# A hybrid attention block with a gated MLP on one core: stick-breaking products moved a chunk behind their transposes, MLP operands combined in rows, first loads of the down product moved into the last up block

## The chip, the core and the metric

The kernel runs on one core of one Trainium2 chip. The core has a tensor engine (TensorE, PE in the profile, with its weight loads shown apart as PEld), a vector engine (VectorE, DVE), a scalar engine (ScalarE, ACT), GpSimd (POOL) and a queue engine (SyncE, SP) which here issues nearly all transfers. The engines run their own instruction lists in order and wait for each other on semaphores. Matrix products land in PSUM, which the kernel uses as eight banks of 128 partitions by 512 float32; everything else on the core lies in SBUF.

The metric is the device time of one execution in microseconds; lower is better. One execution was also recorded by the hardware profiler, and all durations below come from that one.

## What is computed

One decoder layer over 1024 rows of width 1024: a norm, one projection, sparse attention on eight heads and stick-breaking attention on eight others, a norm by head, an output projection with residual, a second norm, a gated MLP with a causal convolution of width 3, and a last norm. The parts that the change touches, cut from the reference:

```python
def _rms_norm(x, w):
    y = xf * lax.rsqrt(jnp.mean(xf * xf, axis=-1, keepdims=True) + EPS)
    return (y * w).astype(x.dtype)
...
def _stick_breaking(q, k, v):            # 8 heads of width 64, T = 1024
    for nb in range(T // QBLK):          # QBLK = 128 rows of q
        z = jnp.einsum('bhqd,bhkd->bhqk', qb, kb) * scale
        log_rest = jnp.where(mask, jax.nn.log_sigmoid(-z), 0.0)
        after = lax.cumsum(log_rest, axis=3, reverse=True) - log_rest
        a = jnp.where(mask, jnp.exp(jax.nn.log_sigmoid(z) + after), 0.0)
        outs.append(jnp.einsum('bhqk,bhkd->bhqd', a, vb))
...
h = h + mixed @ w_out[layer]
u = _rms_norm(h, norm2_w[layer])
up = u @ w_up[layer]                     # 1024 -> 2 x 2816
up = conv_width_3(up, conv_w[layer]) + conv_b[layer]
gate, val = up[..., :D_FF], up[..., D_FF:]
h = h + (jax.nn.silu(gate) * val) @ w_down[layer]
return _rms_norm(h, final_norm_w)
```

## The kernel before

All matrices are float32. A factor is split into a high part (a copy rounded to the reduced type that PE multiplies fast, `fp32r` in the rows) and a low part (factor minus high part), and a product is three matmuls: high by high, high by low, low by high. Splitting a weight is `split_w` (lines 190 to 193): ACT copies, GpSimd subtracts (VectorE for the activations of the down product). Splitting what comes out of a PE transpose is `evac_hl` (lines 180 to 188): ACT copies from PSUM, VectorE subtracts from PSUM.

The code is written as generators that are pulled in turn, so that the work of one stage is emitted between the instructions of another; a scheduler then fixes each engine's order. PSUM tiles have tags: `tr` (two banks, for transposes), `z` (three banks), `o`, `ma` and `mb` (one bank each).

**Stick-breaking attention** (`sb_attend`, lines 367 to 401). There are four pairs of heads, two heads in each, four pairs of row blocks in each head, and the key blocks are cut into chunks of at most four. One turn of the loop pulls `sb_front` of chunk i and `sb_back` of chunk i - 2 (`SB_LAG`), together with projections that serve as filling. `sb_front` makes the logits (lines 422 to 425), ACT takes two sigmoids from the bank, VectorE scans one of them into a running product (line 433) and GpSimd multiplies (line 436) into `A`. `sb_back` takes each pair of key blocks of `A`: four transposes into a `tr` bank (line 463), `evac_hl` into `ph` (ACT, line 184) and `pl` (VectorE, line 185), three buffers each, and then the products with `V` into `o` (lines 453 and 455), in the order ph, pl, ph, pl. The products of one pair of key blocks are emitted after the transposes of the next pair, those of the chunk's last pair after one pull more. When a row block is done, ACT copies `o` (line 481) and `finish` transposes it (line 497) and VectorE reduces the bank into `osb` (line 498). Norms by head come from `head_norm_steps`, whose root is `rstd` (line 162) with `pool` set: GpSimd scales (line 168) and raises to the power -1/2 (line 169).

Right behind it come the blocks of the compressed keys (VectorE line 598, PE line 603) and `project_v` (line 1181), whose raw weights go through the tiles `na` and `nb` of the pool `nt`. The first four raw loads (lines 1192 and 1193) are issued between 19 and 31 us.

**MLP.** The up product is done with seven block products instead of eight, on combinations of the four quarters of its operand (the first and second half of the rows, each by the first and second half of the width): P1 and P2 are the two quarters of rows 0 to 511, and P6, P7, P5, P4 and P3 are sums and differences of quarters. `mlp` (lines 1209 to 1336) does the output projection by row blocks; `row` (line 1268) normalises a row block into a tile `un` (four buffers) without the weight of the norm. `first_half` transposes the first four row blocks (line 1234, eight groups of four transposes), scales by the norm's weight in the copies (lines 187, 188 and 1243) and keeps a float32 copy `bf`. `second_half` has four turns: two groups of transposes, three combinations on VectorE (lines 1255, 1257 and 1259) and one on GpSimd (line 1261), five copies on ACT (line 1264) and five subtractions (line 1265), three on VectorE and two on GpSimd, all from SBUF. It is pulled between the products P1 and P2 of the first three blocks of the up product, the lead products; the rest of the up product runs in `up` (22 blocks, seven products of twelve matmuls each, lines 1392 to 1394).

**Down product** (`down`, lines 1470 to 1567). It goes over two halves of the rows, each with eight banks of sums. The first group has three weight blocks, whose weights and activations are loaded before it; the activations of blocks 0 to 2 use tiles of the up product's pool `gran`. Behind the group the pools of the up product close, the pool `dp` opens in their place, and the loads of block 3 on go there: `ar` for the raw activation (line 1492), `ah` and `al` for its parts. The activation of each up block goes to `act_d` in HBM (line 1423) and is read back from there.

## Time and profile before

| what | us |
|---|---|
| median of three runs (lowest, highest) | 1510.08 (1509.42, 1510.47) |
| the profiled execution, by the same clock | 1511.7 |
| span of its trace, first to last instruction | 1510.0 |
| PE busy in the span | 1440.7 (95%) |
| DVE, ACT, POOL busy | 989.5, 804.8, 776.2 |

The stages by time in the trace: the first norm and projections up to about 60 us, stick-breaking attention with its filling to 372, the projections of the sparse attention to 440, sparse attention to 700, the output projection to 813.6, then a stretch in which the operands of the up product are made while the lead products run, to about 900, the up product to 1258, the down product to 1503 and a tail.

PE busy counts a pipelined matmul from its start to a modelled end, so matmuls of 0.39 us start every 0.23 us when they stand in a row, and a short pause between two does not show as idle time. What PE loses is read from the times at which its matmuls start, from the rows on waits (of PE and of its weight loads), and from the granted clock, which is 1.00 in a stretch at 2.4 GHz and 0.50 at 1.2 GHz.

### The profile page before, as it was taken

How to read it: one execution, taken by the hardware profiler on the slowest of the kernel's cores; microseconds unless marked ns; L12 is line 12 of the kernel's file. 1: busy time of each engine (PE TensorE's matmuls, PEld its weight loads, DVE VectorE, ACT ScalarE, POOL GpSimd, SP SyncE). 2: the span in 40 equal slices, each digit the busy share in tenths (PEclk: the TensorE clock that was granted, in tenths of full speed). 3: DMA queues.
4: the chain of work that ended last, by engine and by line, in shares of the span. 5: the costliest groups of instructions: out<-in, count | busy, mean ns of one | idle time of the engine just before them, and what ended most of it. 6: DMA issues, size and time to landing. Idle time of an engine off the chain costs nothing. (4 is left out here: it accounts for less than half of the span.)

```text
span 1510.0 us, 21800 instructions
## 1 busy us (share of the span) xinstructions
PE 1440.7 (95%) x7571; PEld 1201.5 (80%) x7571; DVE 989.5 (66%) x2013; ACT 804.8 (53%) x1705; POOL 776.2 (51%) x739
## 2 busy tenths in 40 slices
PE   7999999988999999999999799999999999999998
PEld 5777787777987988998888578888888887888886
DVE  5576777676337899998435897777777775614112
ACT  5565666553458888887416444444444453424122
POOL 3344555544336567665133856666666662645043
PEclk8999999999999999999999999999999999999999
DMA  6201101121331010003340122222222223845321
GB/s 208 70 15 28 29 15 28 47 67 53 99 94 29 1 57 2 1 16 105 113 126 35 58 96 79 82 84 85 84 84 84 83 93 130 287 147 181 109 95 56
DMA packets 111402, 119.10 MB, mean 79 GB/s; under 512 B 6860, under 2 KB 84156, under 8 KB 110908
## 3 DMA queue, kind: packets, MB, share of 16 engines
q1 hardware_dynamic: 111292, 117.71, 24.2%
q8 instruction: 60, 0.98, 0.3%
q14 instruction: 50, 0.41, 0.1%
HBM read 93.98 MB, written 23.70 MB: 78 GB/s over the span
## 5 line engine op out<-in xcount | busy, mean ns | idle before, releaser
L436 POOL TENSOR_TENSOR A<-A,tt 128x384 f32<-128x384 f32 (+3 forms) x96 | 90.4, 946 | 125.6 <-DVE tt L433 84.8
L193 POOL TENSOR_TENSOR gl<-mxs,gh 128x512 fp32r<-128x512 f32 x88 | 114.8, 1304 | 61.7 <-ACT gh L192 57.7
L193 POOL TENSOR_TENSOR gl<-wr,gh 128x512 fp32r<-128x512 f32 x66 | 86.1, 1306 | 94.9 <-ACT gh L192 65.8
L193 DVE TENSOR_TENSOR al<-ar,ah 128x512 fp32r<-128x512 f32 x41 | 49.1, 1214 | 126.3 <-ACT ah L192 121.6
L185 DVE TENSOR_TENSOR pl<-ps_tr,ph 128x512 fp32r<-128x512 f32 (+1 forms) x175 | 111.6, 641 | 17.1 <-ACT ph L184 15.4
L193 POOL TENSOR_TENSOR dl<-wr,dh 128x1024 fp32r<-128x1024 f32 x28 | 70.6, 2529 | 98.8 <-ACT dh L192 89.7
L184 ACT ACTIVATE ph<-ps_tr 128x512 fp32r<-128x512 f32 (+1 forms) x175 | 97.8, 563 | 42.6 <-PE ps_tr L463 24.4
L192 ACT ACTIVATE gh<-mxs 128x512 fp32r<-128x512 f32 x91 | 57.3, 629 | 75.6 <-PE ps_ma L1393 22.8
L433 DVE TENSOR_TENSOR_SCAN tt<-tt 128x384 f32<-128x384 f32 (+1 forms) x64 | 67.7, 1061 | 34.2 <-ACT tt L426 33.4
L192 ACT ACTIVATE ah<-ar 128x512 fp32r<-128x512 f32 x41 | 25.7, 629 | 111.2 <-PE ps_ma L1525 101.4
L193 POOL TENSOR_TENSOR wl<-wr,wh 128x512 fp32r<-128x512 f32 x40 | 54.7, 1371 | 50.4 <-ACT wh L192 50.4
L426 ACT ACTIVATE tt<-ps_z 128x384 f32<-128x384 f32 (+3 forms) x96 | 47.8, 497 | 40.3 <-PE ps_z L423 24.2
L692 POOL TENSOR_SCALAR lgw<-lgw,r,gates 128x640 f32<-128x640 f32 (+4 forms) x64 | 48.5, 767 | 39.3 <-DVE r L690 20.8
L192 ACT ACTIVATE gh<-wr 128x512 fp32r<-128x512 f32 x66 | 40.9, 624 | 43.9 <-DMA wr<-w_up_d 15.0
L218 PE MATMUL ps_ma<-uh,wh 128*128 128x512 f32 x136 | 59.4, 437 | 0.3 <-DVE mts L299 0.3
L219 PE MATMUL ps_ma<-ul,wh 128*128 128x512 f32 x136 | 54.7, 402 | 2.8 <-DVE ul L188 2.8
L220 PE MATMUL ps_ma<-uh,wl 128*128 128x512 f32 x136 | 54.2, 398 | 0.0
L463 PE MATMUL ps_tr<-ident,A 128*128 128x128 f32 x320 | 48.2, 274 | 3.8 <-DVE osb L498 3.1
L455 PE MATMUL ps_o<-pl,V 128*128 128x256 f32 x160 | 45.7, 307 | 5.2 <-DVE pl L185 3.3
L218 PE MATMUL ps_mb<-late,wh 128*128 128x512 f32 x120 | 50.4, 420 | 0.0
L463 PEld LDWEIGHTS ps_tr<-ident,A 128*128 128x128 f32 x320 | 37.6, 140 | 13.0 <-DVE osb L498 5.0
L427 ACT ACTIVATE A<-ps_z 128x384 f32<-128x384 f32 (+3 forms) x96 | 47.8, 498 | 0.1
(686 smaller groups left out, 5229.4 us busy)
## 6 DMA issues: line engine op xcount, KB each, us to landing
wr<-w_up_d SPq DMA_DIRECT2D x44, 512.0 KB
wr<-w_down_d SPq DMA_DIRECT2D x36, 512.0 KB
act_d<-na SPq DMA_DIRECT2D x44, 256.0 KB
ar<-act_d SPq DMA_DIRECT2D x41, 256.0 KB
wr<-w_in_d SPq DMA_DIRECT2D x40, 256.0 KB
...
```

The lines of the kernel that those rows point to most:

```text
L184: nc.scalar.activation(hi, src, AF.Copy)
L185: nc.vector.tensor_sub(lo, src, f(hi))
L192: nc.scalar.activation(hi, raw, AF.Copy)
L193: (eng or nc.gpsimd).tensor_sub(lo, raw, f(hi))
L218: nc.tensor.matmul(out, lh, rh, start=(i == 0), stop=False)
L219: nc.tensor.matmul(out, lh, rl, start=False, stop=False)
L220: nc.tensor.matmul(out, ll, rh, start=False, stop=(i == last))
L426: nc.scalar.activation(tt[:, 0:w], z[:, :w], AF.Sigmoid, scale=-1.0)
L433: nc.vector.tensor_tensor_scan(rev, rev, rev, 1.0 if carry[j] is None else carry[j], op0=ALU.mult, op1=ALU.bypass)
L436: nc.gpsimd.tensor_mul(A[:, j, 0:w], A[:, j, 0:w], tt[:, 1:w + 1])
L463: nc.tensor.transpose(pt[:, kk * 256 + j * P:kk * 256 + (j + 1) * P], A[:, j, c0:c0 + P], self.ident)
L692: nc.gpsimd.tensor_scalar(lg[i][:, :L], lg[i][:, :L], r[:, i:i + 1], gate[:, i:i + 1], op0=ALU.mult, op1=ALU.mult)
```

## The change

Nothing is altered in what is computed; the norm's weight is multiplied in another place.

1. *Stick-breaking.* `sb_back` is cut in two: `sb_turn` does the transposes and `evac_hl` of chunk i - 2, and the new `sb_back` does the products of chunk i - 3, all pairs of key blocks of the chunk, in the order ph, ph, pl, pl. `ph` and `pl` have five buffers instead of three, and the loop has one turn more.
2. *MLP operands in rows.* The norm's weight is loaded as a row broadcast to 128 partitions, in the tiles `na` and `nb`; `row` multiplies it in. All eight `un` tiles are kept, `bf` is gone. The new `combine` makes the sums and differences on the row tiles, four subtractions of 128 by 512 on VectorE for each of four pairs of row blocks, in place (one into `mxs`). Every one of the seven operands is then transposed by itself, in four groups of four transposes, each split by `evac_hl` from PSUM: 28 groups of transposes in place of 16. Four groups are pulled between lead products where one turn of `second_half` was.
3. *Down product.* The first group has four weight blocks instead of three. Their weights and activations are loaded within the last up block, the activations' parts into the tiles of P7.

```diff
-        for i in range(len(units) + self.SB_LAG):
+        for i in range(len(units) + self.SB_LAG + 1):
...
+            for lag, step in ((self.SB_LAG, self.sb_turn), (self.SB_LAG + 1, self.sb_back)):
+                if lag <= i < len(units) + lag:
+                    unit = units[i - lag]
+                    p = unit[0]["p"]
+                    gens.append(step(ops[p], work, unit, osb[p], mx, p, aux))
...
-            ph = self.tl(work, [P, 512], "ph", 3, F32R)
-            pl = self.tl(work, [P, 512], "pl", 3, F32R)
+            ph = self.tl(work, [P, 512], "ph", 5, F32R)
+            pl = self.tl(work, [P, 512], "pl", 5, F32R)
             self.evac_hl(ph, pl, pt)
...
+        for k0, ph, pl in u[b1]:
+            yield
+            for half in (ph, pl):
+                for kk in range(2):
+                    nc.tensor.matmul(o[:, :256], V[:, k0 + kk, :], half[:, kk * 256:kk * 256 + 256],
+                                     start=first and k0 == b1 - 2 and kk == 0 and half is ph,
+                                     stop=k0 == 0 and kk == 1 and half is pl)
...
+        w2 = [self.tl(self.nt, [P, 512], t, 2) for t in ("na", "nb")]
...
+        def operand(name, pieces):
+
+            hi, lo = R[name]
+            for k in range(4):
+                pt = self.ps("tr")
+                for j in range(4):
+                    nc.tensor.transpose(pt[:, j * P:(j + 1) * P], pieces(j, k), self.ident)
+                self.evac_hl(hi[:, k, :], lo[:, k, :], pt)
+                yield
...
+        def combine(j):
+
+            (a1, a2), (b1, b2) = ([rows[tb][:, 512 * i:512 * i + 512] for i in range(2)] for tb in (j, 4 + j))
+            nc.vector.tensor_sub(mxs[:, j, :], b1, a1)
+            nc.vector.tensor_sub(b1, b1, b2)
+            nc.vector.tensor_sub(a1, a1, b1)
+            nc.vector.tensor_sub(a2, a2, a1)
...
-            t = rows[tb] = self.tl(unp, [P, DM], "un", 4)
+            t = rows[tb] = self.tl(unp, [P, DM], "un", NB)
...
+            for sv, dv, wv in zip(src, dst, w2):
+                nc.vector.scalar_tensor_tensor(dv, sv, r[:, 0:1], wv, op0=ALU.mult, op1=ALU.mult)
...
-            if n >= 2:
+            for _ in range(4 if n else 0):
                 next(fill, None)
...
+            last = i == NF - 1
+            if last:
+                for _ in range(AHEAD):
+                    self.prepare()
+                self.load_w(0)
+                self.load_w(1)
...
+            if last:
+                for j in range(GROUP):
+                    if j > 1:
+                        self.load_w(j)
+                    self.load_act(j, 0)
...
+        if c == 0 and i < GROUP:
+            raw = self.scratch()
+            ah, al = (t[:, i, :] for t in self.R["P7"])
```

How the order of instructions moves, at three places.

PE in stick-breaking before, at 102 us of the trace: transposes of one pair of key blocks (L463), the products of the pair before them (`ph_1013`, `pl_1014`), a few matmuls of filling (L218 to L220), and then the products of the pair just transposed (`ph_1038`).

```order
L463 MATMUL ps_tr_1033<-ident,A_867 128x128 x4
L453 MATMUL ps_o_940<-ph_1013,V_516 128x256
L455 MATMUL ps_o_940<-pl_1014,V_516 128x256
L453 MATMUL ps_o_940<-ph_1013,V_516 128x256
L455 MATMUL ps_o_940<-pl_1014,V_516 128x256
L218 MATMUL ps_mb_1050<-late_93,wh_907 128x512
L219 MATMUL ps_mb_1050<-late_97,wh_907 128x512
L220 MATMUL ps_mb_1050<-late_93,wl_908 128x512
L453 MATMUL ps_o_940<-ph_1038,V_516 128x256
```

PE in the same part after the change (L454 is the transposes, L474 the products): the products of `ph_1147` and `pl_1148` come from a group of transposes that stands 28 rows further up, and the four transposes shown first serve products 35 rows further down.

```order
L454 MATMUL ps_tr_1220<-ident,A_1046 128x128 x4
L218 MATMUL ps_ma_1200<-uh,wh_1188 128x512
L219 MATMUL ps_ma_1200<-ul,wh_1188 128x512
L220 MATMUL ps_ma_1200<-uh,wl_1189 128x512
L218 MATMUL ps_ma_1200<-uh,wh_1188 128x512
L219 MATMUL ps_ma_1200<-ul,wh_1188 128x512
L220 MATMUL ps_ma_1200<-uh,wl_1189 128x512
L218 MATMUL ps_ma_1200<-uh,wh_1188 128x512
L474 MATMUL ps_o_1199<-ph_1118,V_517 128x256 x2
L474 MATMUL ps_o_1199<-pl_1119,V_517 128x256 x2
L474 MATMUL ps_o_1199<-ph_1147,V_517 128x256 x2
L474 MATMUL ps_o_1199<-pl_1148,V_517 128x256 x2
```

A product that stood eight rows behind its own transposes, four of them products of the pair before, now has 28 or 35 rows between. Counted over all 80 groups in the lists, each PE instruction by the interval at which its kind starts in the trace, the median of PE work between a group's transposes and its first low product (L455; L474 with pl) goes from 2.0 to 7.3 us, and the least from 0.8 to 1.5.

VectorE at the making of the MLP operands before: one turn of `second_half` (`bf` is the float32 copy of the first half, `qn`, `mts` and `P3l` take the low parts) and an instruction of the weights' preparation (L1377).

```order
L1255 SCALAR_TENSOR_TENSOR nb_9858<-ps_tr_9853,cols,na_9851 128x512
L1257 SCALAR_TENSOR_TENSOR na_9860<-ps_tr_9853,cols,bf_9328 128x512
L1259 TENSOR_TENSOR nb_9862<-bf_9328,nb_9858 128x512
L1265 TENSOR_TENSOR P3l_9786<-na_9851,P3h_9785 128x512
L1265 TENSOR_TENSOR mts<-na_9860,mts 128x512
L1265 TENSOR_TENSOR qn<-nb_9862,qn 128x512
L1377 TENSOR_TENSOR mxs<-wr_9579,mxs 128x512
```

VectorE at the same place after: the row block 7 times the norm's weight (L1272 on `h`), its four subtractions of `combine` (L1261 to L1264), the low parts of the first groups of P6 (L185 into `qn`) and a part of the convolution (L1414).

```order
L1272 SCALAR_TENSOR_TENSOR un_9766<-h_9576,ry_9772,nb_9326 128x512
L1261 TENSOR_TENSOR mxs<-un_9766,un_9522 128x512
L1262 TENSOR_TENSOR un_9766<-un_9766 128x512
L1263 TENSOR_TENSOR un_9522<-un_9522,un_9766 128x512
L1264 TENSOR_TENSOR un_9522<-un_9522 128x512
L185 TENSOR_TENSOR qn<-ps_tr_9834,qn 128x512
L185 TENSOR_TENSOR qn<-ps_tr_9841,qn 128x512
L1414 SCALAR_TENSOR_TENSOR na_10072<-ps_ma_9797,cols,na_10072 128x511
L185 TENSOR_TENSOR qn<-ps_tr_9848,qn 128x512
```

The low parts that were subtracted from SBUF to SBUF are subtracted from a PSUM bank, and the combinations stand ahead of the transposes instead of behind them.

SP at the start of the down product before: the last stores of activations (L1423), the reads of the activations of blocks 1 and 2 (L1492 into `mxs`), the weights of block 2 (L1480), and behind the last store the row of the last norm (L1542), the weights of block 3 and the activation of block 3 (`ar`).

```order
L1492 DMA mxs<-act_d_10021 128x512
L1492 DMA mxs<-act_d_10022 128x512
L1480 DMA wr_13455<-w_down_d 128x1024
L1423 DMA act_d_10040<-na_13231 128x512
L1423 DMA act_d_10040<-na_13287 128x512
L1423 DMA act_d_10041<-na_13385 128x512
L1423 DMA act_d_10041<-na_13428 128x512
L1542 DMA fnw_13551<-final_norm_w_d 128x1024
L1480 DMA wr_13553<-w_down_d 128x1024
L1492 DMA ar_13557<-act_d_10023 128x512
```

SP at the same place after (L1503 reads an activation, L1491 a weight, L1429 stores):

```order
L1503 DMA mxs<-act_d_10051 128x512
L1503 DMA mxs<-act_d_10053 128x512
L1503 DMA mxs<-act_d_10052 128x512
L1491 DMA wr_13399<-w_down_d 128x1024
L1491 DMA wr_13406<-w_down_d 128x1024
L1429 DMA act_d_10070<-na_13261 128x512
L1429 DMA act_d_10070<-na_13317 128x512
L1429 DMA act_d_10071<-na_13443 128x512
L1429 DMA act_d_10071<-na_13486 128x512
L1557 DMA fnw_13606<-final_norm_w_d 128x1024
L1491 DMA wr_13608<-w_down_d 128x1024
L1503 DMA ar_13612<-act_d_10054 128x512
```

One activation and one weight block more are read ahead of the last stores, and the first `ar` is that of block 4 instead of block 3. Elsewhere (the projections of sparse attention, sparse attention, the output projection, the up and the down product behind their starts) the lists are the same but for line and tile numbers, with one difference of place: the first four raw loads of `project_v`, ahead of the stick-breaking part's SP work before, stand behind it after, since the wider `ph` and `pl` pools overlap `na` and `nb`.

## Rows read from the trace of the kernel before

**Rows 1.** The page, busy us of each engine over the whole span, its share and its instructions.

```profile
PE 1440.7 (95%) x7571; PEld 1201.5 (80%) x7571; DVE 989.5 (66%) x2013; ACT 804.8 (53%) x1705; POOL 776.2 (51%) x739
```

**Rows 2.** Busy time of each engine by stretch (from and to in us, length, then for PE, its weight loads, DVE, ACT and POOL the busy us and the number of instructions, then the granted clock of TensorE, the DMA share and GB/s).

```profile
60.00:300.00 240.00, 227.94 (x1298) 179.49 (x1296) 168.43 (x305) 154.70 (x332) 126.78 (x149) 1.00 0.11 28
300.00:352.00 52.00, 43.24 (x233) 34.37 (x233) 41.60 (x64) 26.82 (x56) 28.14 (x30) 0.94 0.21 59
...
700.00:822.00 122.00, 121.89 (x620) 100.85 (x619) 57.48 (x106) 52.20 (x106) 30.68 (x38) 1.00 0.32 106
822.00:906.00 84.00, 70.19 (x293) 54.94 (x292) 75.17 (x91) 42.99 (x74) 61.43 (x43) 0.94 0.22 69
906.00:1268.00 362.00, 362.00 (x1598) 299.85 (x1598) 284.25 (x397) 169.67 (x300) 215.99 (x162) 1.00 0.26 82
1268.00:1290.00 22.00, 18.97 (x77) 14.96 (x76) 10.26 (x5) 9.71 (x12) 12.36 (x5) 0.92 0.72 252
```

**Rows 3.** What PE's weight loads waited for between 60 and 300 us (us in total, times, longest); a weight load that starts late holds its matmul.

```profile
PEld ps_o L455 <- DVE pl L185: 7.9, 15, 1.9
PEld ps_tr L463 <- DVE osb L498: 4.8, 4, 2.4
PEld ps_tr L497 <- ACT tt L481: 4.8, 4, 1.9
PEld ps_o L453 <- ACT ph L184: 2.4, 6, 0.8
PEld ps_tr L463 <- DVE pl L185: 1.9, 4, 0.7
PEld ps_o L455 <- DVE tt L429: 1.7, 4, 0.6
```

**Rows 4.** The timeline of all engines around 102 us (start, us, engine, line, operation, tiles; in brackets the idle time before it and its releaser).

```profile
102.00 0.60 PE L463 MATMUL ps_tr<-ident,A 128*128 128x128 f32 x4
...
102.96 0.59 ACT L184 ACTIVATE ph<-ps_tr 128x512 fp32r<-128x512 f32 x1
...
103.61 0.37 PE L453 MATMUL ps_o<-ph,V 128*128 128x256 f32 x1
...
104.16 0.69 DVE L185 TENSOR_TENSOR pl<-ps_tr,ph 128x512 fp32r<-128x512 f32 x1
...
104.91 0.39 PE L455 MATMUL ps_o<-pl,V 128*128 128x256 f32 x1 [0.22 <-DVE pl L185]
```

**Rows 5.** What PE waited for between 300 and 352 us (us in total, times, longest).

```profile
PE ps_ma L603 <- DVE blk L598: 6.1, 3, 3.9
```

**Rows 6.** The timeline of PE in the output projection: one group of four transposes and the matmul behind it.

```profile
795.49 0.60 PE L1234 MATMUL ps_tr<-ident,un 128*128 128x128 f32 x4
795.85 0.48 PE L961 MATMUL ps_z<-w,mts 128*128 128x512 f32 x1
```

**Rows 7.** What PE waited for between 790 and 900 us (us in total, times, longest).

```profile
PE ps_z L1393 <- DVE qn L1265: 4.4, 2, 3.2
PE ps_tr L1234 <- DVE na L1257: 4.1, 2, 3.4
PE ps_tr L1392 <- DVE mxs L1441: 2.1, 1, 2.1
```

**Rows 8.** Groups of DVE's instructions by line and shape between 820 and 906 us (count, busy us, mean ns of one, idle time before them).

```profile
L1265 DVE TENSOR_TENSOR P3l<-na,P3h 128x512 fp32r<-128x512 f32 x4 | 7.1, 1771 | 0.0
L1265 DVE TENSOR_TENSOR mts<-na,mts 128x512 fp32r<-128x512 f32 x4 | 7.1, 1767 | 0.0
L1265 DVE TENSOR_TENSOR qn<-nb,qn 128x512 fp32r<-128x512 f32 x4 | 7.0, 1758 | 0.0
...
L1259 DVE TENSOR_TENSOR nb<-bf,nb 128x512 f32<-128x512 f32 x4 | 4.4, 1104 | 0.0
...
L1255 DVE SCALAR_TENSOR_TENSOR nb<-ps_tr,cols,na 128x512 f32<-128x512 f32 x4 | 3.0, 745 | 6.3 <-ACT na L1251 6.2 <-issue 0.2
```

**Rows 9.** The timeline around 1250 us: a subtraction on POOL, and two on DVE of the kind of L1265, the first beside it and the second with POOL idle.

```profile
1247.84 2.84 POOL L193 TENSOR_TENSOR qn<-wr,qn 128x1024 fp32r<-128x1024 f32 x1
...
1248.95 2.29 DVE L193 TENSOR_TENSOR gl<-mxs,gh 128x512 fp32r<-128x512 f32 x1
...
1251.76 0.67 DVE L193 TENSOR_TENSOR gl<-mxs,gh 128x512 fp32r<-128x512 f32 x1
```

**Rows 10.** The timeline of DVE for the last row block at the end of the output projection: the addition of the residual and the second scaling.

```profile
814.13 0.69 DVE L1302 TENSOR_TENSOR h<-ps_z,h 128x512 f32<-128x512 f32 x1
...
817.17 0.48 DVE L1179 TENSOR_SCALAR un<-h,ry 128x512 f32<-128x512 f32 x1
```

**Rows 11.** The timeline of all engines at the start of the down product, behind its first group.

```profile
1273.70 0.33 SPq L1492 DMA_DIRECT2D ar<-act_d  x1
...
1276.88 0.63 ACT L192 ACTIVATE ah<-ar 128x512 fp32r<-128x512 f32 x1 [4.62 <-DMA ar<-act_d]
...
1277.57 0.59 PE L1524 MATMUL ps_o<-qn,ah 128*128 128x512 f32 x1 [3.03 <-ACT ah L192]
...
1278.88 0.63 PE L1524 MATMUL ps_z<-qn,ah 128*128 128x512 f32 x1
```

**Rows 12.** The timeline at the end of stick-breaking: the root of a head's norm on POOL, and the first split of `project_v` on ACT.

```profile
374.37 1.64 POOL L169 TENSOR_TENSOR ry<-rv,mhalf 128x8 f32<-128x8 f32 x1
...
377.16 0.44 ACT L192 ACTIVATE wh<-na 128x280 fp32r<-128x280 f32 x1 [6.57 <-POOL mxs L321]
```

198 lines of the change are left out of this document (78 added, 120 removed).

## The prediction

> **What bounds the kernel now.** I read the busy times first [rows 1]: PE is at work 1440.7 of 1510.0 us, all others at two thirds or less. So PE sets the time, and an edit is worth what it takes from PE's instructions or from PE's pauses. Then the stretches [rows 2]: the reader is to see that PE is full in the output projection (121.89 of 122) and in the up product (362.00 of 362), so nothing can be won there, and that it has holes in four places: 12.1 us between 60 and 300, 8.8 between 300 and 352, 13.8 between 822 and 906, 3.0 between 1268 and 1290. In the last three the granted clock is also below 1 (0.94, 0.94, 0.92): part of each runs at the lower level, 1.2 GHz, behind a pause. Then, for each hole, the rows on what ended last: VectorE's low parts and ACT's copies in stick-breaking [rows 3], VectorE at the compressed keys [rows 5] and at the MLP operands [rows 7], a transfer at the down product [rows 11].
>
> The "roots on GpSimd" of the change's name are no part of its difference: the root of a head's norm is an instruction of POOL before already (1.64 us [rows 12]). I count it as nothing.
>
> **Stick-breaking.** No matmul is removed: the same 80 groups of transposes, the same 320 products. What goes is the closeness of a product to its own transposes. The chain of one group [rows 4]: transposes at 102.00, ACT's copy at 102.96 (it had other work first), the low part at 104.16 (VectorE too), product at 104.91: 2.9 us, where PE had less than that between. With the change the median of work between is 7.3 us and the least 1.5, so a chain of 2.9 is covered nearly everywhere but in the last turns.
> The price: between 60 and 300 us weight loads waited 7.9, 2.4 and 1.7 us for products (25 waits), 4.8 for the transposes of a finished row block (4) and 4.8 + 1.9 for a free `tr` bank (8) [rows 3]. A weight load of 0.19 us runs ahead of its matmul, so I take 0.19 off each wait: products 12.0 - 25 x 0.19 = 7.3; row blocks 4.8 - 0.8 = 4.0; banks 6.7 - 1.5 = 5.2. The products' waits go whole. The row blocks' wait is for ACT's copy of `o`, which follows the last product; it now stands a chunk further from its transposes, and I take 80% of it, 3.2. The banks' wait I leave: there are still two `tr` banks and VectorE's list has the same work in it. Sum **10.5 us**. Bounds: 3 (the waits pass to the banks) and 16.5 (all three go).
> The 6.1 us for `blk` [rows 5] stay: VectorE's own work there is unmoved (41.60 busy of 52 us [rows 2]).
> A cost: the four first raw loads of `project_v` now stand on SP behind the last low product of stick-breaking, about 370 us, with the store of the attention output and the gates' bias behind them. ACT splits the first of them at 377.16, and it waited there 6.57 us for POOL, not for the load [rows 12]. So seven us cover a load, and I take 0; without that cover PE has other projections to run for some 15 us more, so the bound is 3.
>
> **The MLP operands.** Before: between 822 and 906 PE was idle 13.8 us, and 6% of 84 us of clock is missing, 5.0 [rows 2]: 18.8. Counted otherwise: 293 instructions stand there, 32 of them transposes of 0.36 us a group of four (795.49 to 795.85 [rows 6]), the rest matmuls that start every 0.2275 when in a row: 8 x 0.36 + 261 x 0.2275 = 62.3, so 21.7 of 84 were lost. I take 20. VectorE is the cause: three low parts of 1.77 each, a difference of 1.10 and two of 0.74 in each of four turns, back to back [rows 8], and PE waits for a low part, for the last read of a `tr` bank, and for the weights' sums queued behind [rows 7].
> Removed: the twelve low parts from SBUF on VectorE, 21.2 us, and POOL's twelve. Added: 28 low parts from PSUM where 8 were, at 0.69 [rows 4], 13.8 us; sixteen subtractions, of which twelve run beside the output projection while PE is full, and four behind it; and 12 groups of transposes more on PE, 12 x 0.36 = **4.3 us, all on the path**.
> New waits. First: the last row block leaves the output projection at 813.6, its residual is added at 814.13 and its second scaling starts at 817.17 [rows 10], now a product with the weight's row (0.75 in place of 0.48, by the form with a tensor from PSUM [rows 8]); then four subtractions at 0.67 (POOL idle) to 1.77 (POOL beside) [rows 8, 9], and only then can a P6 group be transposed, at about 821 to 825. PE has the second half of P1's lead product, three groups' pieces and P2's to run meanwhile, up to about 821: 1 us of waiting.
> The Trainium skill ("SBUF — State Buffer", "SBUF: two separate sides") has a VectorE operation with two SBUF inputs and a GpSimd operation that reads SBUF exclude each other for a whole instruction. The 2.29 us beside POOL against 0.67 alone [rows 9] agree. By that rule the weight's row and the four subtractions, all with two SBUF inputs, could each stand behind one of POOL's weight subtractions; the sum by it is the third rival's, below.
> Second: twenty groups follow, with two `tr` banks. A bank's round is 0.36 + 0.59 + 0.69 [rows 4, 6] and three handovers, about 2.1 us by estimate from these rows, so a group every 1.05; PE has 5 lead products x 12 x 0.2275 = 13.7 us to spread over them, 0.68 + 0.36 = 1.04 a group. They are even, and with ACT's copies for the convolution in between I take 0.2 a group: 4 us. No long pause is left, so I let the clock stay at 2.4 GHz.
> Sum: 20 - 4.3 - 1 - 4 = **10.7 us**. Bounds: 4 (a round of 2.9 as in rows 4: 1.45 a group, 8 us of waiting for 4, and the first wait at 4) and 15.
>
> **The down product.** The first group ended and PE stood 3.03 us for the activation of block 3: its transfer was issued at 1273.70, behind the group's end, since its place was held by a tile that PE still read, and ACT copied it at 1276.88 [rows 11]. The clock then fell: a matmul at 1278.88 took 0.63 for 0.39 [rows 11], and 8% of 22 us, 1.8, is missing [rows 2]. With block 3 in the first group its activation is read before the last stores, and the raw load of block 4 needs a place that comes free early. But the low part of block 4 (`al`) lies over P7's tiles, which PE reads until the group ends; VectorE can write it only then: 0.67 alone to 2.29 beside POOL [rows 9], less two matmuls that need no low part (0.46): 0.2 to 1.8 us. I take 0.8. 3.0 + 1.8 - 0.8 = **4.0 us**, bounds 2 and 4.7. The weights and activations brought into the last up block load VectorE and ACT at a place where both have room (284 and 170 of 362 [rows 2]); uncovered, a late one costs what is counted as the lower bound.
>
> **Sum.** 10.5 + 10.7 + 4.0 = 25.2. The profiled execution took 1511.7 (span 1510.0 and 1.7 around it), so 1486.5 for one like it; the median of the runs before is 1.6 lower than that execution, which gives **1485 us**.
>
> **Rivals.**
> *The stalls of stick-breaking only move.* VectorE and ACT do the same work in the same order of chunks, and PE is then held by the `tr` banks instead of the products. For it: 6.7 us of waits are for banks already [rows 3]. Against it: VectorE is busy 168 of 240 [rows 2], no bound. Stick-breaking gives 2.5 for 10.5: 1493.
> *Two `tr` banks pace the transposes.* For it: 28 groups for 16, and the round of 2.9 in rows 4. Four us more of waiting, and a pause behind which the clock falls (1.8 as at the down product): 1491. The Trainium skill ("Perfetto Trace Analysis", "Matmuls") asks that matmul groups rotate through banks so that evacuation overlaps; two banks for twenty groups is little of that.
> *VectorE is late with the last row block.* Five operations with two SBUF inputs at 1.77 for 0.67, 5.5 us more, nearly all of it a pause of PE: 1490.5. Against it: POOL's work on the operands is gone, only the weights' is left. The rule of the Trainium skill ("SBUF — State Buffer", "SBUF: two separate sides") would make this of it.
> *Slower.* All transposes of a chunk are now emitted without products between, so a bank can be asked for before VectorE, in order and behind a scan, has emptied it. The eight bank waits of before average 6.7 / 8 = 0.84 us [rows 3]. If N of 80 groups wait so long, stick-breaking pays 0.84 N - 6.7; it decides from 0.84 N - 6.7 = 7.3 + 3.2 + 10.7 + 4.0, N = 38. At N = 55: 1510 - 14.7 - 10.5 + 39.5 = 1524. Against it: PE's work between a group and the next but one hardly changes.
>
> **How the numbers follow.** A difference of 0.2%, 3 us, is about what a measurement of this kernel can tell. Forecast, each part giving half or more: 0.60, 1474 to 1496. Stalls move 0.13, banks pace 0.10, VectorE late 0.06; two of these together reach 1499 and stay faster. Slower 0.05. The rest, 0.06, is a gain lost by something no row shows, within 0.2%. Faster 0.89, same 0.06, slower 0.05. Range: up to two or three rivals at once, 1502, down to all three upper bounds at once, 16.5 + 15 + 4.7 = 36.2, so 1474.
>
> **What would show it.** Right: hardly a wait of PE for `ph` or `pl` in stick-breaking; a granted clock near 1 between 822 and 880, with VectorE no longer full and PE's waits there under 0.6 us each; no pause over 1 us at the down product's second group; the stretch of 300 to 352 as before. Wrong: `tr` waits of the sum that the products had, PE waiting for the first P6 group over 3 us, or a first 128x280 product of `project_v` that waits for its load.

## The result, and the profile after

| | median us | range, executions |
|---|---|---|
| before | 1509.75 | 1508.68 to 1510.47, 4 |
| after | 1502.28 | 1499.37 to 1504.82, 4 |

The ratio is 0.995, interval 0.9931 to 0.997: the change gains 7.5 us, where 25 were forecast. The direction was right; the time lies 0.3 us above the upper end of the range. The four executions after are wider apart than those before and go with the granted clock (0.991, 0.989, 0.988 and 0.987 for 1499.37, 1501.84, 1502.73 and 1504.82). The profiled one is the fastest of them, 12.3 us under the profiled one of before, so its rows show 12.3 us of gain where the medians show 7.5.

The page, busy us of each engine; it answers [rows 1].

```profile
PE 1435.7 (96%) x7619; PEld 1204.5 (80%) x7619; DVE 989.5 (66%) x2025; ACT 796.7 (53%) x1693; POOL 756.5 (51%) x727
```

The 48 transposes more are there (7619 matmuls for 7571), and PE is still the bound. The same by stretch, moved to where the work stands now; it answers [rows 2].

```profile
60.00:290.00 230.00, 220.60 (x1290) 178.96 (x1288) 174.25 (x303) 153.18 (x329) 126.70 (x149) 1.00 0.12 30
290.00:342.00 52.00, 44.74 (x241) 36.18 (x240) 42.35 (x67) 27.42 (x56) 27.52 (x29) 0.93 0.21 60
690.00:810.00 120.00, 118.06 (x606) 97.82 (x604) 67.18 (x116) 46.25 (x96) 29.39 (x34) 1.00 0.34 110
810.00:892.00 82.00, 73.81 (x343) 59.09 (x344) 61.98 (x91) 39.71 (x72) 41.88 (x32) 0.96 0.21 65
895.00:1257.00 362.00, 361.49 (x1595) 299.03 (x1594) 286.26 (x400) 171.30 (x303) 220.58 (x164) 1.00 0.26 83
1257.00:1279.00 22.00, 20.39 (x91) 16.56 (x90) 6.67 (x6) 8.13 (x10) 10.41 (x5) 1.00 0.69 240
```

Three things are to be seen. The first stretch does its work in 230 us for 240. At the operands VectorE went from 75 of 84 us to 62 of 82, as forecast, and yet PE still stands 8.2 us there and 4% of the clock is missing, where it was to be near 1. The start of the down product (last row) keeps its clock.

Which part gained what is read best from leads. The table gives, for a kernel's profiled execution, the time at which PE starts a given instruction less the time of the same one in before: the first logits (64.7 us in before), a product of the projections behind stick-breaking (458.7), the last product of the output projection (813.7), the 301st matmul of the up product with its leads (907.2), its last (1257.8), the last of the down product (1502.1). Negative is earlier; a difference between neighbouring columns is what that stage gained. The other kernels are told further down.

| kernel | 64.7 | 458.7 | 813.7 | 907.2 | 1257.8 | 1502.1 |
|---|---|---|---|---|---|---|
| after | -1.6 | -9.0 | -7.8 | -9.9 | -9.1 | -12.2 |
| after_again | -1.5 | -9.6 | -8.5 | -13.0 | -10.9 | -13.8 |
| sb_only | -0.3 | -7.8 | -7.5 | -9.0 | -9.0 | -9.1 |
| mlp_only | -0.3 | 0.0 | +0.8 | -3.0 | -3.0 | -5.4 |
| down_only | -0.1 | -1.2 | -0.6 | -0.5 | +0.3 | -2.7 |
| o2 | -0.2 | -9.6 | -8.1 | -11.1 | -9.1 | -10.3 |
| ot | +1.2 | -11.9 | -10.6 | -12.8 | -12.0 | -14.8 |
| pool | -0.5 | -8.1 | -7.2 | -12.0 | -11.2 | -14.2 |
| banks | -0.1 | -7.6 | -7.0 | -15.3 | -13.3 | -16.1 |
| actpool | -0.2 | -7.4 | -6.6 | -7.8 | -7.8 | -11.5 |
| late | 0.0 | -6.8 | -3.6 | -6.3 | +1.0 | +0.1 |
| late16 | +0.1 | -6.5 | -4.8 | -7.4 | -0.3 | -1.2 |
| shift | -0.1 | -6.5 | -4.7 | -6.9 | +2.0 | +0.7 |
| pad128 | +1.3 | -5.6 | -2.8 | -7.1 | -0.5 | -1.6 |
| late_rt | +0.6 | -6.8 | -5.8 | -14.0 | -13.2 | -16.2 |
| best | -0.1 | -13.8 | -12.2 | -19.2 | -12.6 | -14.4 |
| best2 | -0.5 | -14.4 | -12.8 | -19.5 | -19.5 | -22.7 |
| best3 | +1.1 | -11.2 | -9.5 | -17.0 | -17.0 | -20.7 |
| best4 | +1.2 | -11.1 | -9.7 | -16.9 | -16.9 | -20.8 |

How far such a difference can be trusted is seen where a kernel has nothing changed in a stage: sb_only gains 1.5 at the operands, down_only 1.1 in stick-breaking. One kernel taken twice is further apart at the operands: 2.1 in after and 4.5 in after_again; the granted clock cost 1.7 more in after, and one wait was 1.1 longer. So one or two us are scatter, and at the operands up to two and a half.

**Stick-breaking** gains 7.4 in after (from -1.6 to -9.0) for 10.5 forecast. The products' waits went as foreseen, and a new one came. What weight loads waited for between 60 and 290 us, after; it answers [rows 3].

```profile
PEld ps_o L474 <- ACT tt L483: 6.0, 9, 1.7
...
PEld ps_tr L454 <- DVE pl L185: 2.7, 6, 0.7
PEld ps_tr L454 <- POOL A L438: 2.4, 2, 1.9
```

No product waits for `ph` or `pl` any more. But the first product of a row block (L474) now waits for ACT's copy of the row block before (L483), which frees the one bank `o`. In the last row blocks it costs most. What PE waited for between 290 and 440 us, after; the first row answers [rows 5]:

```profile
PE ps_ma L605 <- DVE blk L600: 5.2, 3, 2.1
PE ps_o L474 <- ACT tt L483: 3.7, 1, 3.7
```

The timeline of GpSimd, ACT and PE there:

```profile
338.83 1.05 POOL L168 TENSOR_SCALAR rv<-hss 128x8 f32<-128x8 f32 x1 [0.25 <-DVE tt L431]
...
339.96 1.64 POOL L169 TENSOR_TENSOR ry<-rv,mhalf 128x8 f32<-128x8 f32 x1
...
341.68 1.80 POOL L321 TENSOR_TENSOR mxs<-osb,ry 128x512 f32<-128x512 f32 x1
...
343.45 3.42 POOL L438 TENSOR_TENSOR A<-A,tt 128x512 f32<-128x512 f32 x2
...
346.90 0.38 ACT L483 ACTIVATE tt<-ps_o 128x256 f32<-128x256 f32 x1 [3.98 <-POOL A L438]
...
347.34 0.58 PE L474 MATMUL ps_o<-ph,V 128*128 128x256 f32 x1 [3.69 <-ACT tt L483]
```

The copy of `o` is put into one of the four `tt` buffers. GpSimd still reads that buffer in its multiply, and the multiply stands behind the root and the scaling of a head's norm. ACT waits 3.98 us for a place to write, and PE 3.69 for the bank.

**The operands** gain 2.1 (from -7.8 to -9.9) for 10.7. What PE waited for between 785 and 900 us, after; it answers [rows 7].

```profile
PE ps_tr L1240 <- DVE un L1263: 3.7, 2, 2.6
PE ps_tr L1240 <- DVE P4l L185: 3.0, 1, 3.0
PE ps_tr L1398 <- ACT na L1427: 1.9, 1, 1.9
PE ps_tr L1240 <- DVE qn L185: 0.6, 1, 0.6
PE ps_z L1398 <- ACT na L1427: 0.3, 1, 0.3
```

The 0.6 lies at 790 us, still in the output projection; the 1.9 and the 0.3 are not waits of transposes but of the up product's own matmuls on P4, at 867 and 881 us. The transposes have two long pauses, of 2.6 (behind a first one of 1.1) and 3.0 us. The clock behind them, in stretches of 10 us (columns as in rows 2):

```profile
810.00:820.00 10.00, 7.02 (x29) 5.54 (x30) 8.60 (x12) 3.91 (x8) 3.44 (x4) 0.91 0.07 26
820.00:830.00 10.00, 10.00 (x56) 7.93 (x56) 5.50 (x9) 7.46 (x13) 2.57 (x2) 0.92 0.00 0
830.00:840.00 10.00, 7.00 (x39) 5.40 (x38) 6.76 (x9) 4.34 (x8) 4.17 (x3) 0.93 0.37 107
840.00:850.00 10.00, 10.00 (x51) 8.10 (x51) 5.44 (x9) 4.74 (x9) 5.04 (x4) 0.90 0.18 52
```

The missing tenths are 0.9 + 0.8 + 0.7 + 1.0 = 3.4 us. That sum is not fixed: in after_again, with the same 2.6 us pause and 1.9 for `P4l`, it is 1.7. The first pause, in VectorE's list with the last row block, after; it answers [rows 10]:

```profile
806.60 1.78 DVE L1261 TENSOR_TENSOR mxs<-un,un 128x512 f32<-128x512 f32 x1
...
809.02 0.68 DVE L1303 TENSOR_TENSOR h<-ps_z,h 128x512 f32<-128x512 f32 x1
...
812.04 1.77 DVE L1272 SCALAR_TENSOR_TENSOR un<-mxs,ry,na 128x512 f32<-128x512 f32 x1 [0.94 <-POOL ry L169]
...
815.85 1.63 DVE L1263 TENSOR_TENSOR un<-un,un 128x512 f32<-128x512 f32 x1
```

The residual of row block 7 (L1303) stands among the sums of the row blocks 2 and 6 (L1261 to L1264), two of them ahead of it and two behind, and three operations with two SBUF inputs took 1.63 to 1.78 us where the same lines also show 0.68 to 0.75; GpSimd was at work beside each (from 806.15, 811.98 and 815.49). The second pause:

```profile
834.77 1.28 POOL L1377 TENSOR_TENSOR mxs<-wr 128x512 f32<-128x512 f32 x1 [5.62 <-DMA wr<-w_up_d]
...
836.09 1.73 DVE L1378 TENSOR_TENSOR mxs<-mxs,wr 128x512 f32<-128x512 f32 x1 [2.25 <-POOL mxs L1377]
...
837.74 0.68 DVE L185 TENSOR_TENSOR P4l<-ps_tr,P4h 128x512 fp32r<-128x512 f32 x1
...
838.48 1.03 PE L1240 MATMUL ps_tr<-ident,un 128*128 128x128 f32 x4 [3.00 <-DVE P4l L185]
```

A weight's difference (L1378) that waits for a transfer and for GpSimd stands on VectorE ahead of the low part that frees the bank.

**The down product** gains 3.1 for 4.0: the pause is 1.61 us, and the clock stays at 1.00. It answers [rows 11].

```profile
1270.73 4.93 DVE L193 TENSOR_TENSOR al<-ar,ah 128x512 fp32r<-128x512 f32 x2 [13.32 <-PE ps_ma L1533]
1272.92 0.19 PEld L1534 LDWEIGHTS ps_o<-mts,al 128*128 128x128 f32 x1 [2.03 <-DVE al L193]
1272.92 0.50 PE L1534 MATMUL ps_o<-mts,al 128*128 128x512 f32 x1 [1.61 <-DVE al L193]
```

### The profile page after: what moved, and what is told of

The parts are those of the page before. It is cut to its first block, busy times and chain, and to the rows that moved or that the text cites. A ratio compares the mean times of both kernels' runs of the same rounds, so it can differ in the third digit from the quotient of the medians.

```text
span 1497.4 us, 21900 instructions
## 1 busy us (share of the span) xinstructions
PE 1435.7 (96%) x7619; PEld 1204.5 (80%) x7619; DVE 989.5 (66%) x2025; ACT 796.7 (53%) x1693; POOL 756.5 (51%) x727
## 5 line engine op out<-in xcount | busy, mean ns | idle before, releaser
L193 DVE TENSOR_TENSOR al<-ar,ah 128x512 fp32r<-128x512 f32 x40 | 42.0, 1060 | 128.4 <-ACT ah L192 110.2
L185 DVE TENSOR_TENSOR pl<-ps_tr,ph 128x512 fp32r<-128x512 f32 (+1 forms) x175 | 112.1, 643 | 16.5 <-ACT ph L184 14.7
L218 PE MATMUL ps_ma<-uh,wh 128*128 128x512 f32 x136 | 59.0, 434 | 0.0
L454 PE MATMUL ps_tr<-ident,A 128*128 128x128 f32 x320 | 48.8, 275 | 6.3 <-DVE pl L185 4.3
L220 PE MATMUL ps_ma<-uh,wl 128*128 128x512 f32 x136 | 53.9, 397 | 0.0
L218 PE MATMUL ps_mb<-late,wh 128*128 128x512 f32 x120 | 50.5, 421 | 0.0
L454 PEld LDWEIGHTS ps_tr<-ident,A 128*128 128x128 f32 x320 | 36.9, 141 | 16.0 <-issue 4.9
L1427 ACT ACTIVATE na<-na 128x512 f32<-128x512 f32 x44 | 27.6, 628 | 39.9 <-DVE na L1423 39.9
L1378 DVE TENSOR_TENSOR mxs<-mxs,wr 128x512 f32<-128x512 f32 x22 | 35.3, 1606 | 19.8 <-POOL mxs L1377 19.7
```

What stands on the lines that cost most here:

```text
L185: nc.vector.tensor_sub(lo, src, f(hi))
L193: (eng or nc.gpsimd).tensor_sub(lo, raw, f(hi))
L218: nc.tensor.matmul(out, lh, rh, start=(i == 0), stop=False)
L454: nc.tensor.transpose(pt[:, kk * 256 + j * P:kk * 256 + (j + 1) * P], A[:, j, c0:c0 + P], self.ident)
```

## The experiments

Each was timed in five rounds beside the kernel before, whose median was 1510.7 to 1510.9 in all of them. Diffs are against after; those of the first three kernels are parts of the diff under the change.

### The parts alone, and the whole again

**sb_only**, **mlp_only** and **down_only** are the kernel before with one part of the change (numbered 1, 2 and 3 above); **after_again** is the changed kernel timed beside them.

> The kernel before with the stick-breaking part of the change alone (products a chunk later, five buffers of ph and pl). The theory of the prediction, that the products' waits go and nothing comes in their place: 10.5 us less than before, about 1499.5. The rival formed on the trace after, that the products now wait for the one bank of o, which ACT still copies: about 6 us less in the stretch of stick-breaking, 1504, and weight-load waits of the products for ACT's copy of o of some 16 us where the kernel before has 0.6. If the 1.6 us that the trace after shows before 63 us come from the four raw loads of project_v that no longer run there, they show in this kernel too; if not, they are scatter of one execution.

> The kernel before with the MLP operands made in rows alone. The prediction: 10.7 us less, about 1499. The rival formed on the trace after, that pauses of PE for the last row block's sums (3.7 us) and for the low part of P4 (3.0 us), each with a stretch at the lower clock behind it, take the place of those removed, and 48 transposes more are paid: 1 to 2 us less, about 1508.5.

> The kernel before with the first loads of the down product in the last up block and a first group of four alone. The prediction: 4.0 us less (2 to 4.7), 1506. By the trace after, where PE waits 1.6 us for the low part of block 4: 3.0 us less, 1507. If the gain needed the other parts of the change, nothing.

> The changed kernel itself, beside its three parts on one chip. If the parts don't touch each other, its gain is the sum of theirs: by the prediction 25, by the trace after 11 to 12, by the runs so far 7.5. If the runs so far are right and the profiled execution was a good one, single times scatter here by several us where the kernel before scatters by one or two.

| kernel | median | ratio | gain |
|---|---|---|---|
| sb_only | 1504.25 | 0.9954 (0.9942 to 0.9967) | 6.5 |
| mlp_only | 1506.38 | 0.9971 (0.9961 to 0.9982) | 4.3 |
| down_only | 1509.24 | 0.999 (0.9981 to 0.9999) | 1.5 |
| after_again | 1501.25 | 0.9935 (0.9921 to 0.9948) | 9.5 |

Each part is a gain and none gives what was forecast. The parts add to 12.3 for 9.5. The table of leads shows why: mlp_only gains 2.4 at the start of the down product, which it doesn't edit, since PE's pause there is 1.9 us with the clock at 1.00, where before had 3.0 and 0.92. So that gain is counted twice. What made its activation come earlier was not followed up.

### Stick-breaking: the bank of `o`, or the tile it is copied into

**o2** gives `o` two banks during stick-breaking, the second one taken from the three of `z`:

```diff
+                self.zsplit, self.alias = True, dict(self.alias, o=["o", "zx"])
                 for _ in self.sb_attend(start, work, mxs):
```

**ot** leaves the banks and gives the copy two tiles of its own:

```diff
-        ot = self.tl(work, [P, 513], "tt", 4)[:, 0:256]
+        ot = self.tl(work, [P, 256], "ot", 2)
```

> The changed kernel with two banks for o in stick-breaking, taken from the three of the logits z, which keep two. The theory that the products wait for ACT's copy of the one bank of o: their waits for that copy (16 us before weight loads, 10 us more than the shortest interval before the first product of a row block in the trace after) go, and stick-breaking takes 6 to 9 us less than in the changed kernel: about 1494. The rival, that VectorE and ACT pace this part and a wait only moves on: the waits come back before the logits' matmuls or the transposes, and the time stays within 2 us of 1501.

> The changed kernel with tiles of their own (two of 128 by 256) for ACT's copy of o, which takes one of the four tiles of the scan (tt) otherwise. The trace after shows the copy late by 4.0 us at 346 us, waiting for GpSimd's multiplication that still reads a tt tile, behind the head norm's root and scaling on GpSimd; PE stands 4.8 us. The theory that the single bank of o is held mostly by that: the last pause goes and stick-breaking keeps the 3 us that it gives back behind 340 us, 2 to 4 us less than the changed kernel, 1498. The rival that the bank itself, with ACT's own queue, is what holds: the waits for the copy stay at 11 us or more in sum, within 1 us of 1501.

o2: 1497.18, ratio 0.9917 (0.9903 to 0.9931). ot: 1495.93, ratio 0.9896 (0.9881 to 0.9912), 5.3 us under after_again. From the first logits to 458.7 us, o2 gains 9.4 and ot 13.1; the eleven kernels of the table with the new stick-breaking and neither edit gain 6.4 to 8.1. GpSimd and ACT at the same place in ot:

```profile
341.74 3.49 POOL L438 TENSOR_TENSOR A<-A,tt 128x512 f32<-128x512 f32 x2
...
344.68 0.38 ACT L483 ACTIVATE ot<-ps_o 128x256 f32<-128x256 f32 x1
```

The copy now runs beside the multiply, and the row of L474 for `tt` is gone from the waits. With two banks the copy's wait for `tt` passes to the transposes of the finished row block, 2.8 us of their weight loads in o2. So the bank is where the wait is felt, and the shared tile is most of its cause: from the first logits to 458.7 us the second bank alone gained 1.3 over after_again, the tiles 5.0. The interval of ot lies clear of that of after_again; o2's overlaps it.

### The operands: banks, and what stands ahead on VectorE

**banks** lets the operands' transposes rotate through five banks, two of `tr` and three of `z`:

```diff
+        self.alias = {"tr": ["tr", "tr", "z", "z", "z"]}
         fill = second_half()
```

**pool** puts the weights' differences of P6 and P3 of the first two blocks on GpSimd:

```diff
-                nc.vector.tensor_sub(v, s1, raw(0)[0])
+                (nc.gpsimd if i < 2 else nc.vector).tensor_sub(v, s1, raw(0)[0])
```

(and the same for the other one). **late** takes the residual and the scaling of row block 7 ahead of the sums of the row blocks 2 and 6; a factor 1.0, made from row block 7 on GpSimd, holds those sums back:

```diff
+            nc.vector.scalar_tensor_tensor(mxs[:, j, :], b1, one, a1, op0=ALU.mult, op1=ALU.subtract)
+            nc.vector.scalar_tensor_tensor(b1, b1, one, b2, op0=ALU.mult, op1=ALU.subtract)
...
+                if tb == 7:
+                    one = self.st([P, 2], "one", 1)[:, 0:1]
+                    nc.gpsimd.tensor_scalar(one, h1[7][:, 0:1], 0.0, 1.0, op0=ALU.mult, op1=ALU.add)
+                    combine(2, one)
+                    combine(3)
```

> The changed kernel with five banks for the operands' transposes (the two of tr and the three of z, which the lead products don't use). The rival of the prediction, that two banks pace twenty groups: 3 to 4 us less than the changed kernel, 1497.5, and PE no longer waits for a low part of an earlier group. The theory that VectorE's order makes the two long pauses: the first pause (for the last sums) stays, and less than 2 us are won.

> The changed kernel with the weights' differences for P6 and P3 of the first two up blocks on GpSimd instead of VectorE. The theory that PE's pause of 3.0 us before a P4 group (and the lower clock behind it) is a low part that stands on VectorE behind a difference of weights, which itself waits 2.25 us for GpSimd's sum: 3 to 5 us less than the changed kernel, 1497. The rival: GpSimd is late with them then, and a lead or first product waits for its weights instead; within 1 us of 1501.

> The changed kernel with the sums of row blocks 2 and 6 tied behind the residual addition of row block 7, so that VectorE starts the last row block right at the end of the output projection and not 2.8 us later. The theory that PE's first pause (1.1 + 2.6 us for the sum of row block 3, and a stretch at 1.2 GHz behind it) comes from VectorE's order there: 3 to 5 us less than the changed kernel, 1497. The rival of two tr banks pacing the transposes: under 1 us less, since the same groups then wait for their banks.

banks: 1496.68, ratio 0.9911 (0.9897 to 0.9924). pool: 1497.44, ratio 0.9912 (0.9899 to 0.9925). late: 1510.69, ratio 0.9995 (0.9986 to 1.0004). PE's waits in banks, 785 to 900 us:

```profile
PE ps_z L1240 <- DVE un L1263: 3.7, 2, 2.6
PE ps_tr L1400 <- ACT na L1429: 1.9, 1, 1.9
PE ps_tr L1240 <- DVE qn L185: 0.6, 1, 0.6
PE ps_z L1240 <- DVE P4l L185: 0.2, 1, 0.2
```

The wait for `P4l` goes from 3.0 (1.9 in after_again) to 0.2, and the operands gain 8.3 us for 2.1 in after and 4.5 in after_again. Not all of that is the edit's: the first pause is as long as ever, and yet the clock stays at 1.00 in each 10 us from 810 to 850, where after_again lost 1.7 us of it. Of the 3.8 us between banks and after_again 1.7 are the wait and 1.7 the clock. The wait in after_again, and two of the stretches (columns as in rows 2), of after_again and then of banks:

```profile
PE ps_tr L1240 <- DVE P4l L185: 1.9, 2, 1.6
```

```profile
810.00:820.00 10.00, 7.37 (x33) 5.75 (x32) 8.39 (x11) 3.60 (x7) 3.45 (x4) 0.90 0.06 21
820.00:830.00 10.00, 10.00 (x57) 8.11 (x56) 5.29 (x8) 7.55 (x14) 2.58 (x2) 0.93 0.03 9
```

```profile
810.00:820.00 10.00, 6.31 (x35) 5.14 (x35) 8.59 (x12) 3.75 (x8) 3.45 (x4) 1.00 0.07 26
820.00:830.00 10.00, 10.00 (x62) 8.69 (x61) 7.72 (x13) 8.79 (x17) 2.57 (x2) 1.00 0.11 31
```

In pool the wait is 0.5 and 1.7 us of clock are lost. The intervals of both kernels just touch that of after_again, so it is the waits that decide. Both edits reach the same pause, one from each side: either the bank is not needed so soon, or VectorE is not stopped ahead of it. So two `tr` banks did hold the transposes up, at this one place, which was a rival. The Trainium skill ("Perfetto Trace Analysis", "Matmuls") asks that matmul groups rotate through banks so that evacuation overlaps; this run agrees: the wait is gone, and the time is 4.6 us less, with the clock in it. The first wait, 3.7, stands.

late lost its time elsewhere: 7.3 us between 907 and 1258 us, in a product that no edit touches.

### The slower up product

In late the matmuls of the up product started 231 ns apart instead of 226.7. Its new tile of 8 bytes takes 32, and the tiles behind the small ones (weights, P7, P4, P3) stand 32 bytes further, while `qn` and `mts` stay. **late16** is late with a tile of 64 bytes.

> The same as late, but its helper tile is 64 bytes wide instead of 8, so that all tiles behind it move by 64 bytes and not by 32. In late each 128x512 matmul of the up product started 231 ns after the one before, against 226.7 in every other kernel, and its weights' tiles were the only ones not at a multiple of 64 bytes. If that is the cause, the interval is 226.7 again here and the kernel gains the 8 us that late lost; then the theory on VectorE's order at the last row block can be read: 1 to 3 us less than the changed kernel, 1499. If the interval stays at 231, the cause is another, and 1510.

late16: 1508.58, ratio 0.9985 (0.9971 to 0.9999), 231 ns. So 64 bytes don't mend it. **shift** takes the edit away and keeps only a tile that nobody reads, written once; **pad128** makes it 128 bytes; **late_rt** keeps the order of late and puts its factor into a buffer that is there already (the second diff, against late):

```diff
+                    nc.gpsimd.memset(self.st([P, 16], "pad", 1), 0.0)
```

```diff
-                    one = self.st([P, 2], "one", 1)[:, 0:1]
+                    one = self.st([P, 16], "rv", 4)[:, 0:1]
```

> The changed kernel with one tile of 64 bytes more in the pool of small tiles, written once by GpSimd during the output projection and read by nobody; every instruction else is the same. If the 231 ns between matmuls of the up product in the two kernels with the row-7 order come from the place of the tiles that lie behind the small ones: 230 to 232 ns here too, and 1505 to 1510 us. If they come from the edited instructions or the order of VectorE: 226.7 ns and 1501 (1499 to 1504).

> The row-7 order once more (the last row block's residual and scaling ahead of the sums of the pair before), with the helper value in a buffer of a tile that is there already, so that no tile moves. If the tiles' place made the 231 ns: 226.7 ns in the up product, the first wait of PE for the P6 group 2.8 us for 3.7, and 1500 (1498 to 1502). If the edit itself made them: 231 ns and 1507 to 1511.

> The changed kernel with an unused tile of 128 bytes in the pool of small tiles, where the run before had one of 64. In the list of addresses the weights, P7, P4 and P3 stand at multiples of 128 bytes in the changed kernel, 32 bytes off one in the first kernel with the row-7 order, 64 off one in the second and in the one with the 64-byte tile, and at multiples of 128 here again. If the boundary is what counts: 226.7 ns in the up product and 1501 (1498 to 1504). If any move of these tiles against the others (the operands on the right side stay) counts: 231 ns and 1508 to 1513.

shift: 1512.36, ratio 1.0006 (0.9996 to 1.0016). pad128: 1509.42, ratio 0.999 (0.9981 to 0.9999). late_rt: 1495.32, ratio 0.9891 (0.9876 to 0.9906). The same 280 us of the up product in after_again, and then in shift (columns as in rows 2):

```profile
920.00:1200.00 280.00, 280.00 (x1237) 231.90 (x1237) 220.19 (x312) 132.48 (x237) 173.00 (x133) 1.00 0.28 85
```

```profile
920.00:1200.00 280.00, 280.00 (x1214) 227.14 (x1213) 217.11 (x302) 129.80 (x232) 172.41 (x131) 1.00 0.26 79
```

PE is full and at full clock in both, and does 1214 matmuls for 1237. pad128 does 1216, late_rt 1237. So the edit is cleared, and the place of the tiles is shown to be the cause: 11 us for an unused tile. Not every matmul pays. In shift those on `qn` and `mts`, which did not move, start 233.3 ns apart on average; those on P3, which moved together with the weights, stay at 226.7, and those on P4 and P7, which moved too, stay there but for the first five of each twelve. So it is the place of one factor against the other that counts, and not that of a tile by itself. Why, is open: shifts of 32, 64 and 128 bytes are all slow, and the last of these keeps every boundary of up to 128 bytes, so it is none of those.

late_rt is what late was to be. It gains 8.2 at the operands, with these waits:

```profile
PE ps_tr L1240 <- DVE un L1263: 2.5, 2, 2.2
...
PE ps_tr L1240 <- DVE P4l L185: 0.9, 2, 0.6
```

and a granted clock of 1.00 in each 10 us from 810 to 870. The first wait fell only from 3.7 to 2.5. Its operands beat those of after_again by 3.7 us. Three terms make that up to within the scatter: that wait (1.2), the one for `P4l`, which shrank with VectorE's list in another order (1.0), and the clock (1.7).

### The last up block

**actpool** puts the low parts of the first four activations on GpSimd:

```diff
-        self.split_w(raw, ah, al, self.nc.vector)
+        self.split_w(raw, ah, al, None if c == 0 and i < GROUP else self.nc.vector)
```

> The changed kernel with the low parts of the first four activations of the down product on GpSimd instead of VectorE. In the last up block VectorE takes 6 us for these four, and PE then waits 0.5 to 1.5 us for sums that stand behind them. The theory that the early loads cost that much of their own gain: the last up block takes 1 to 2 us less, 1500. The rival: GpSimd, which splits the weights there too, is late with the first activation and the down product starts later by as much; no change.

1499.37, ratio 0.9924 (0.9911 to 0.9936): 1.9 under after_again, with overlapping intervals, so the times alone don't show it. The leads do: between 907 and 1258 us actpool, best2, best3 and best4, which have this edit, give back nothing; the kernels with the early loads, without this edit and with 226.7 ns a start give back 0.8 to 2.1 (after_again 2.1). What PE waited for there in after_again, and the largest group on VectorE at the end of the up product (1225 to 1262 us) in the same kernel:

```profile
PE ps_ma L1398 <- DVE ps_tr L1462: 1.1, 1, 1.1
PE ps_tr L1398 <- DVE mxs L1453: 0.4, 1, 0.4
```

```profile
L193 DVE TENSOR_TENSOR P7l<-mxs,P7h 128x512 fp32r<-128x512 f32 x4 | 6.0, 1529 | 0.2 <-ACT P7h L192 0.2
```

Four low parts of 1.5 us stand ahead of operations that PE waits for. In actpool no wait is listed.

### All together

**best** is ot, banks, actpool and late16; **best2** is ot, banks and actpool; **best3** is best2 with the order of late_rt; **best4** is best2 with the edit of pool.

> The changed kernel with four of these edits together: the copies' own tiles, five banks for the operands' transposes, VectorE's order at the last row block, and the activations' low parts on GpSimd. If each works on a pause of its own, they add: 3 for the copies, 4 for the banks, 1 to 2 for the order, 1 for the low parts, about 1491. If the pauses only hand over to each other, no better than with the banks alone, 1496.7.

> Three edits that each showed where the forecast gain went, in one kernel: ACT's copy of o in two tiles of its own, five banks for the transposes of the operands, the low parts of the first four activations on GpSimd. Alone they gave 5.3, 4.6 and 1.9 us against the changed kernel's 1501.25. If they act at three different places, as the theory has it, they add: 1489.5 (1487 to 1492), with no pause of PE over 1.5 us for ACT's tt in the last row blocks and none over 1 us for P4's low part, and 226.7 ns from matmul to matmul in the up product. If the gains overlap, or the single kernels' times were scatter, 1494 to 1497, no better than the best of them.

> The three edits of the first kernel of this call with the row-7 order, the helper value in a tile that is there already. By the theory of the tiles' place: 1488.5 (1486 to 1491), a microsecond below the kernel without the row-7 order, with 226.7 ns in the up product. If the row-7 order itself slows the up product: 1495 to 1498 and 231 ns. If the first wait is set by something else than the order of the sums: no difference from the kernel without it.

> The kernel with the three edits (own tiles for o, five banks, activations' low parts on GpSimd; 1489.3) and the weights' differences of P6 and P3 on GpSimd for the first two blocks. Alone the last edit gave 3.8 us, by taking away PE's wait for P4's low part, which the five banks have taken away already (0.3 left in that kernel). If that is all it does: 1489 (1487 to 1491), no gain. If VectorE's list as a whole bounds the operands: the first wait of 3.7 shrinks, and 1485 to 1487.

| kernel | median | ratio |
|---|---|---|
| best | 1497.30 | 0.9915 (0.9902 to 0.9927) |
| best2 | 1489.26 | 0.9856 (0.9843 to 0.987) |
| best3 | 1490.99 | 0.9869 (0.9856 to 0.9883) |
| best4 | 1490.60 | 0.9865 (0.9852 to 0.9879) |

best2 beats both kernels: 21.7 us under the kernel before. The single gains 5.3 + 4.6 + 1.9 = 11.8 against after_again give 12.0 together, as they would from three separate places, and the leads show them there. best loses 6.6 in the up product by its tile's place. best3 and best4 are no better than best2: once there are five banks, neither the order nor a lighter VectorE gives anything more that can be measured. In best3 the order did take the first wait down to 1.7, but the one for `P4l` is back at 1.7; in best4 the first wait is 3.8. The operands in best2, columns as in rows 2:

```profile
805.00:887.00 82.00, 76.53 (x364) 62.67 (x365) 63.94 (x96) 40.72 (x75) 44.24 (x34) 0.98 0.24 74
```

## Why the prediction was wrong

The steps that failed are three: the sum put the bank of `o` in stick-breaking at nothing, where it cost 6.0 us of weight loads and a pause of 3.7; it put the clock at the operands at nothing, where 3.4 us were lost; and it priced the first wait for P6 at 1 us, where it was 3.7. The table below goes by the profiled executions. Between these two the gain is 12.3, 4.9 more than between the medians: 2.0 because the profiled execution of before is above its median, 2.9 because that of after is its fastest, with a granted clock of 0.991 for 0.989 and 0.988 in the two middle ones. No trace shows where those two lost it. By its own steps, in us of gain, from the leads:

| step | forecast | after | best2 |
|---|---|---|---|
| start | 0 | 1.6 | 0.5 |
| stick-breaking | 10.5 | 7.4 | 13.9 |
| up to the end of the output projection | 0 | -1.2 | -1.6 |
| operands | 10.7 | 2.1 | 6.7 |
| rest of the up product | 0 | -0.8 | 0.0 |
| down product | 4.0 | 3.1 | 3.2 |

- *Stick-breaking.* The products' waits went whole, as said, and so did the wait of a finished row block's transposes for ACT's copy (4.8 before, no row of it after up to 290 us). The step that failed stands behind "I take 80% of it, 3.2": the copy did get further from its transposes, but the first product of the next row block now stands closer behind it and needs the bank that it frees, a cost that the sum put at nothing. That wait was 6.0 us in nine weight loads up to 290 us and 3.7 more for PE at the end. None of the rivals had it: in the first of them the stalls move to the `tr` banks, and those waits stayed small (2.7 in 6 up to 290 us), so the slower rival, made of them, did not come either. The copy's tile is shared with GpSimd's multiply; with its own tile the term is over its forecast, inside its bounds of 3 to 16.5.
- *Nothing for the late raw loads.* No wait for a load shows in the listed waits between 290 and 440 us, so 0 was right.
- *The operands* hold most of the miss. The mechanism was right (VectorE unloaded, the twelve low parts gone); what failed are two sizes and one cost put at nothing. "1 us of waiting" for the first P6 group was 3.7: the row block's operations stood beside GpSimd and behind another pair's sums; the prediction had named over 3 us there as a sign of being wrong. "0.2 a group: 4 us" for the banks was 3.0, not spread but in one pause, and the up product's own matmuls on P4 waited 2.2 more for ACT, as some did before, for which the sum had no term. "No long pause is left, so I let the clock stay" was wrong: 3.4 us are missing behind two pauses. Together 2.7 - 1.0 + 2.2 + 3.4 = 7.3 of the 8.6 missing. The last of these is in part chance: the same kernel lost 1.7 in after_again, and banks, with the same first pause, nothing. The rival of the two banks is borne out by banks, which took 4.6 us less with part of that from the clock; it was priced at 6 with a chance of 0.10. The rival of the late VectorE is half right: three operations beside GpSimd took 1 us more each. The rule of the Trainium skill it came from ("SBUF — State Buffer", "SBUF: two separate sides") agrees with the 1.63 to 1.78 us, but the pause it was to make is 2.6, not 5.5.
- *The last up block* is "a place where both have room" taken over the whole up product, and not in its last 20 us, where four low parts stood ahead of what PE needed. 0.8 to 2.1 us, shown by the leads of the kernels with and without the edit of actpool.
- *The down product* was right, with the wait for `al` at the upper end of its 0.2 to 1.8, longer than the 1 us that the prediction's signs allowed: GpSimd ran beside it (2.47 us each, half of 4.93).
- *The range* went as far as two or three rivals at once, 1502. What came was short at four places at once, at two of them (the bank of `o`, the last up block) by causes that were no rival. That 1502.28 lies so near to 1502 is chance.

Left open: why the tiles' place slows matmuls; what sets the first wait for P6, 3.7 us in best2 too, of which the order took away 1.2 (late_rt) to 2.0 (best3) and the lighter VectorE nothing; why one and the same pause costs clock in one execution and not in another; and some 1 us of the output projection.
